# State-space layer: tokens reach rows (step, channel) and leave them through device memory in 256-byte runs; output products with the tables stationary

## The chip, the core and the metric

The kernel runs on one core of a Trainium2 chip. The time is that of one launch on the device, in microseconds (us). Before the change it is 2755.4 us, the median of three runs (2751.41, 2755.40 and 2757.46).

## What is computed

Two layers work on 1024 tokens of 1024 channels, in float32: RWKV-7 time mixing with its MLP, then an S5 state-space layer with its MLP. After each of the four parts the result is `layer_norm(sqrt(2) * h + f(h))`. The part around the change is the state-space layer: 64 groups of 16 channels, each of which drives 64 complex states by a diagonal recurrence.

```python
# s5_mix, cut: u is (token, group g, channel c), s a complex state per (group g, p)
s[t] = abar * s[t-1] + einsum('gc,gpc->gp', u[t], bbar)
y[t] = einsum('gp,gcp->gc', s_re[t], c_re) - einsum('gp,gcp->gc', s_im[t], c_im)
y = gelu(y + x * d_skip)
z = y @ w_glu
return z[..., :d] * sigmoid(z[..., d:])
```

## The kernel before

Activations lie channel-major: a tile holds 128 channels by 512 tokens, eight tiles `h[0..7]` make one half of the sequence, and the two halves are called A (H = 0) and B (H = 1). Each dense product is made of three float32r matmuls (`mm3`; all appear as L188 in the profile): a weight piece of 128 x 512 numbers is loaded into `wraw` (two buffers), copied by ScalarE into `whi`, and its remainder is made by VectorE in `wlo` (three buffers each; L148 and L149 are the helper lines of this split). One such piece is the stationary operand of four steps of the contraction, three matmuls each with `whi` or `wlo`.

The program is written as a sequence of Python calls with ranks; a planner orders each engine's instructions by rank and by a simulated time line. Every engine then takes its own queue strictly in that order. All DMAs are issued from the queue of SyncE (SP). Low ranks go first: layer norms have 99000, the state-space layer has 99300 (half A) and 99400 (half B), the building of its tables has 99500, and the dense MLPs have ranks from 200000 up. So the MLP of one half fills TensorE while the state-space layer of the other half goes through its chain:

1. `s5_tables` (L1010) makes three tables in device memory, interleaved with the first MLP: `tB` (input to state, per step), `tC` (state to output) and `tT` (input to output inside a block of eight steps). `tT` comes from `kpad`, a zero-padded tile of 16 taps, of which a window shifted by the step is stored.
2. `layer_norm(hA, 1, 0)` and then `s5(0, hA)`; the filler is `mlp(0, 1, hB)`, of which 12 of 16 steps stand ahead of `glu(0, hA)` in the program.
3. `layer_norm(hB, 1, 1)` and `s5(1, hB)`; the filler is `mlp(1, 0, hA)`, of which 13 steps stand ahead of `glu(1, hB)`.

Inside `s5` a half of 512 tokens is seen as 64 blocks of SL = 8 steps. The products want rows (step, channel): 8 steps x 16 channels of one group on 128 partitions, with the 64 blocks along the free axis. That form, `ug`, is reached by two rounds of transposes on TensorE. The first (`turn`, L154 for the upper and L156 for the lower half of the output) takes every eighth column of `h` and fills `u1` through `pu1` (copied at L1172). The second (L1179) turns each group of `u1` and is copied into `ug` at L1181. Then `pbu` (L1190) multiplies with `tB` into `hb`, and `advance` (L1200 to L1206, on VectorE and GpSimd) runs the recurrence over the blocks.

The output products have the tokens stationary: at L1234 `ug` (128 rows x 64 blocks) is the stationary operand and 128 columns of `tt` move, read with a step of four elements; at L1239 `hb` (64 rows x 64 blocks) is stationary and 128 columns of `tcm` move. The result has blocks on partitions, is copied to `y1` (L1241) and turned back to channels by a third round of transposes (`pyt`, L1247). VectorE adds `d * h` (L1249, in and out with a step of eight), ScalarE applies the gelu (L1251) and the tile is stored (L1252, `scr["y"]`). `glu` loads it again (L930) and splits it into operands for two dense products per output tile; L1000 and L1001 form the gated sum in `h`.

Elsewhere, `gate_c` in the first layer uses a constant tile `pick` (two 128 x 128 selectors; L355 to L360), and `h` comes from rings of eight buffers (`htile`).

In the profile one fp32 matmul appears as two records, each with its own weight load (PEld); a transpose made with `PE.transpose` appears as one.

Of the kernel before, what the change touches and what calls it, by code (L numbers as in the profile page):

```python
# [8 lines left out]
F32 = mybir.dt.float32  # L9
# [9 lines left out]
HT = 512  # L19
KT = 8  # L20
# [12 lines left out]
TB = 2  # L33
LN8R = 400000
# [36 lines left out]
def trunk(ctx, tc, A):  # L71
# [165 lines left out]
    pick = cp.tile([128, 2, 128], F32, name="pick")  # L237
    for j in range(2):
        V.tensor_copy(pick[:, j].rearrange("p (q n) -> p q n", q=4),
                      ident[:, 64 * j : 64 * j + 32].unsqueeze(1).broadcast_to([128, 4, 32]))  # L240

    def rwkv_proj(H):
# [9 lines left out]
        for k in range(KT):  # L252
            t = ap.tile([128, HT + 1], F32, tag="xs", name="xs", bufs=8)
# [95 lines left out]
        def gate_c():  # L349
# [3 lines left out]
            S.copy(e, p)  # L353
            p = psd()
# [472 lines left out]
    def htile(H):  # L827
        if H == 0:
            return ap.tile([128, HT + 1], F32, tag="xs", name="hA", bufs=8)[:, 0:HT]
        return sp.tile([128, HT], F32, tag="hB", name="hB", bufs=8)  # L830

    def layer_norm(h, gi, H, split_out=True):
# [41 lines left out]
        for k, t in enumerate(h):  # L874
            V.tensor_mul(t, t, pr)
            S.activation(t, t, AF.Identity, bias=vec(b, k), scale=vec(g, k))
            if split_out:
                ops.append(operand(t, H, G if k in LNG else V))
# [112 lines left out]
    def glu(H, h):  # L991
        ys = yload(H)
        for n in range(KT):
# [7 lines left out]
            V.scalar_tensor_tensor(h[n], h[n], ALPHA, s, op0=ALU.mult, op1=ALU.add)  # L1001
# [4 lines left out]
    tT = dr.tile([KT, 128, 2, 512], F32, name="tT")  # L1006
# [3 lines left out]
    def s5_tables():  # L1010
# [78 lines left out]
        kpad = pp.tile([128, 16, 16, 4], F32, name="kpad")  # L1089
        G.memset(kpad, 0.0)  # L1090
        for f in range(KT):
# [18 lines left out]
            def expand(out, src, npow, neg):  # L1110
# [15 lines left out]
            expand((ca[:, :, 0], ca[:, :, 1]), (bc[:, 1, 0], bc[:, 1, 1]), 9, True)  # L1126
            expand((bp[:, :, 0], bp[:, :, 1]), (bb[:, 0], bb[:, 1]), 8, False)
# [9 lines left out]
            for par in range(2):  # L1137
                ps_ = slice(64 * par, 64 * par + 16)
                S.copy(kpad[ps_, 8:].rearrange("p t c g -> p g (t c)"), p[ps_])
            tv = tT[f].rearrange("(s c) two n -> two c s n", c=16)  # L1140
            for par in range(2):
                src = kpad[64 * par : 64 * par + 16, 1:9].rearrange("p t c g -> p (t c g)")
                SP.dma_start(tv[par], bass.AP(src.tensor, src.offset, [src.ap[0], (64, SL), src.ap[1]]))
# [13 lines left out]
    def s5(H, h):  # L1157
# [6 lines left out]
        for f2 in range(4):  # L1164
            u1 = s5p.tile([128, 8, SL, 16], F32, tag="u1", name="u1", bufs=2)
# [214 lines left out]
```

## Time and profile before

| | |
|---|---|
| median of three runs | 2755.4 us |
| the profiled execution | 2756.91 us |
| its span, first to last instruction | 2755.1 us |
| mean granted TensorE clock | 0.958 |
| PE / PEld busy | 94% / 76% |
| DVE / ACT / POOL busy | 66% / 42% / 23% |
| PE's share of the chain that ended last | 63% |
| DMA: packets, volume | 215058, 345.90 MB |
| packets under 512 B | 21184 |

A group of instructions in the profile reads: line, engine, operation, output<-inputs, for a matmul rows*columns of the stationary operand, then out<-moving shape, xcount | busy time in us, mean ns of one | idle time of the engine just before them and what ended it. "SPq" is the queue that issues the DMAs. A matmul's record contains its latency, so records overlap; the busy time of a group is the union of its records.

### The profile page before, as it was taken

The numbers are of one execution on the slowest core, as the hardware profiler recorded it, in microseconds if no ns is written. First come the engines' busy times: TensorE is split into PE (matmuls) and PEld (weight loads), VectorE is DVE, ScalarE is ACT, GpSimd is POOL, SyncE is SP. The second block draws the span as 40 slices with busy tenths as digits, with TensorE's granted clock in tenths as the row PEclk, the third lists the DMA queues.
The fourth block names the chain that finished last, engine by engine and source line by source line (L and its number), as shares of the span: only waits on it lengthen the run. The fifth ranks groups of instructions, "written<-read, shape, count | busy, mean of one in ns | idle before, by whom it ended". The sixth has DMA issues, their size and how long they took to land.

```text
span 2755.1 us, 43773 instructions
## 1 busy us (share of the span) xinstructions
PE 2602.8 (94%) x16582; PEld 2099.3 (76%) x16582; DVE 1811.4 (66%) x3191; ACT 1156.3 (42%) x2038; POOL 628.2 (23%) x515
## 2 busy tenths in 40 slices
PE   7999879899899999889999999999999999999997
PEld 5778767678777877667877788778778887788886
DVE  7477676477788767997658554574765546855556
ACT  7455574554453333344432332344223324433333
POOL 3120642341334212332122000120220001210101
PEclk9989979899879999999999999999999999999999
DMA  4765455465222334564233533233343332333333
GB/s 146 234 206 164 153 180 153 148 192 170 87 79 83 99 94 145 138 157 140 89 123 118 185 96 98 83 89 106 113 164 112 98 96 85 115 96 97 97 94 103
DMA packets 215058, 345.90 MB, mean 126 GB/s; under 512 B 21184, under 2 KB 75584, under 8 KB 214848
## 3 DMA queue, kind: packets, MB, share of 16 engines
q1 hardware_dynamic: 214848, 343.10, 40.2%
q8 instruction: 131, 2.15, 0.3%
q14 instruction: 79, 0.65, 0.1%
HBM read 279.06 MB, written 63.96 MB: 125 GB/s over the span
## 4 chain that ended last, share of the span: by engine, by line
PE 63%; DVE 12%; DMA 5%; issue 4%; ACT 2%; POOL 1%; SPq 0%; ACTq 0%; DVEq 0%; POOLq 0%
PE d L188 53%; DVE wlo L149 2%; DMA wraw<-in_mw_dram 2%; PE py L1234 1%; PE pA L580 1%; PE py L1239 1%; DMA yl<-s_y 1%; DVE hA L975 1%; PE pbu L1190 1%; PE pu L154 1%; PE pR L687 1%; PE pX L692 0%; POOL rl L959 0%; ACT whi L148 0%; DVE t L1202 0%
## 5 line engine op out<-in xcount | busy, mean ns | idle before, releaser
L148 ACT CAST whi<-wraw 128x512 fp32r<-128x512 f32 x668 | 413.6, 620 | 932.0 <-PE d L188 625.0
L149 DVE TENSOR_TENSOR wlo<-wraw,whi 128x512 fp32r<-128x512 f32 x668 | 497.8, 746 | 432.6 <-ACT whi L148 412.7
L188 PE MATMUL d<-qbuf,whi 128*128 128x512 f32 (+1 forms) x2112 | 655.0, 393 | 20.5 <-DVE hA L975 7.7
L188 PEld LDWEIGHTS d<-qbuf,whi 128*128 128x128 f32 x2112 | 390.7, 190 | 115.2 <-DVE hA L975 14.6
L188 PE MATMUL d<-qbuf,wlo 128*128 128x512 f32 (+1 forms) x1056 | 409.5, 390 | 9.5 <-DVE wlo L149 9.3
L188 PE MATMUL d<-oAh,whi 128*128 128x512 f32 (+1 forms) x960 | 394.4, 414 | 21.0 <-ACT ev L417 8.4
L959 POOL TENSOR_TENSOR rl<-rl 128x512 f32<-128x512 f32 x128 | 155.7, 1216 | 1084.4 <-ACT rl L958 1080.4
L188 PE MATMUL d<-oAl,whi 128*128 128x512 f32 (+1 forms) x960 | 390.6, 408 | 5.6 <-DVE oAl L149 5.6
L188 PE MATMUL d<-oAh,wlo 128*128 128x512 f32 (+1 forms) x960 | 390.2, 407 | 5.8 <-DVE wlo L149 3.4
L188 PE MATMUL d<-oBh,whi 128*128 128x512 f32 x704 | 278.6, 396 | 0.0
L188 PE MATMUL d<-oBh,wlo 128*128 128x512 f32 x704 | 277.7, 395 | 0.0
L188 PE MATMUL d<-oBl,whi 128*128 128x512 f32 x704 | 276.4, 393 | 0.0
L188 PEld LDWEIGHTS d<-qbuf,wlo 128*128 128x128 f32 x1056 | 200.0, 190 | 55.1 <-DVE wlo L149 13.6
L188 PEld LDWEIGHTS d<-oAh,whi 128*128 128x128 f32 (+1 forms) x960 | 188.0, 196 | 66.5 <-ACT ev L417 10.2
L188 PEld LDWEIGHTS d<-oAh,wlo 128*128 128x128 f32 (+1 forms) x960 | 188.2, 196 | 49.9 <-DVE wlo L149 5.1
L188 PEld LDWEIGHTS d<-oAl,whi 128*128 128x128 f32 (+1 forms) x960 | 188.4, 196 | 46.9 <-DVE oAl L149 7.8
L975 DVE TENSOR_TENSOR hB<-hB,d 128x512 f32<-128x512 f32 (+1 forms) x256 | 165.2, 651 | 70.7 <-PE d L188 67.9
L975 DVE TENSOR_TENSOR hA<-hA,d 128x512 f32<-128x512 f32 x240 | 162.3, 683 | 47.1 <-PE d L188 44.2
L188 PEld LDWEIGHTS d<-oBh,wlo 128*128 128x128 f32 x704 | 132.5, 188 | 32.1 <-issue 2.0
L188 PEld LDWEIGHTS d<-oBl,whi 128*128 128x128 f32 x704 | 132.6, 188 | 29.9 <-issue 0.9
L188 PEld LDWEIGHTS d<-oBh,whi 128*128 128x128 f32 x704 | 132.8, 189 | 28.2 <-issue 0.7
L149 DVE TENSOR_TENSOR qbuf<-rl,qbuf 128x512 fp32r<-128x512 f32 x128 | 95.7, 748 | 73.0 <-ACT qbuf L148 72.6
(373 smaller groups left out, 3818.1 us busy)
## 6 DMA issues: line engine op xcount, KB each, us to landing
wraw<-in_mw_dram SPq DMA_DIRECT2D x520, 256.0 KB, 2.7
wraw<-in_glu_dram SPq DMA_DIRECT2D x64, 256.0 KB, 2.6
low<-wlo SPq DMA_DIRECT2D x52, 256.0 KB, 2.7
wlo<-low SPq DMA_DIRECT2D x52, 256.0 KB, 3.5
wraw<-in_wk_dram SPq DMA_DIRECT2D x32, 256.0 KB, 3.6
wraw<-in_wr_dram SPq DMA_DIRECT2D x32, 256.0 KB, 3.6
wraw<-in_wv_dram SPq DMA_DIRECT2D x32, 256.0 KB, 4.2
yl<-s_y SPq DMA_DIRECT2D x32, 256.0 KB, 3.1
```

What stands on the lines that cost most here:

```text
L148: S.copy(hi, src)
L149: (e or V).tensor_sub(lo, src, hi.bitcast(F32))
L154: PE.matmul(out, x, idt, start=True, stop=True)
L188: bulk.append((PE.matmul(p, w, x, **kw).ins, x.shape[-1]))
L580: PE.matmul(pp[h][:, cc, i], D.KB[j][hs, u].rearrange("p j l -> p (j l)"), D.AR[j][hs, u].rearrange("p j l -> p (j l)"), start=True, stop= ...
L687: hop.append(PE.matmul(pR[hs, i], at[:, h, c, i, 0], vsa[:, cl, h, i], start=True, stop=True))
L959: G.tensor_mul(r, r, r)
L975: V.tensor_add(z, z, p)
L1190: PE.matmul(p[qs, g2, ri], tb[:, g2, ri, qs], u[:, 2 * g2 + par], start=True, stop=True)
L1234: PE.matmul(p[64 * j : 64 * j + 64, g2], ug[f][:, 2 * g2 + par], tv[:, par, g2], start=g2 == 0, stop=False, skip_group_check=True)
L1239: PE.matmul(p[64 * j : 64 * j + 64, g2], hb[qs, 4 * f + g2, ri, 0:NSC], tcm[qs, g2, ri], start=False, stop=ri == 1, skip_group_check=True)
```

## The change

- **Into rows (step, channel).** The layer norm ahead of `s5` (new argument `steps`) writes each normalised tile to a new buffer with its columns in order (step, block) instead of (block, step), and stores it to `tH` in device memory, eight stores of 256 KB per half. `s5` loads `ug` from there: per tile of four `f`, eight DMAs (one per step), each of 16 partitions x 32 runs of 64 numbers, which is 256 bytes. The transposes of L154, L156 and L1179 and the copies of L1172 and L1181 are gone.
- **Output products.** The tables are stationary: `tt` with 128 x 128, `tcm` with 64 x 128 for each parity; 64 columns of `ug` or `hb` move. The parities go to two PSUM banks.
- **Out of the rows.** Two copies per `f2` put the result into `y` (16 x 64 per partition), and eight DMAs store it to `tY`, each of 16 partitions x 16 runs of 256 bytes. The transposes of L1247 are gone; `d * h` and the gelu move into `glu`, on tiles in order (step, block). `glu` ends with one strided instruction per tile, into a new buffer, that restores the order of tokens.
- **Tables.** `tT` is laid out by partition, written from a larger `kpad` (four `f` together) by 16 DMAs for every four `f` (32 in all, 16 before) in runs of 512 bytes; the powers used for `tB` are taken in reversed order from `pwr`, eight small copies on ScalarE.
- **Buffers.** The rings of `h` have nine buffers; `pick` is no constant but is made in `gate_c`, each time, in a `wraw` buffer.

```diff
-    pick = cp.tile([128, 2, 128], F32, name="pick")
...
-            t = ap.tile([128, HT + 1], F32, tag="xs", name="xs", bufs=8)
+            t = ap.tile([128, HT + 1], F32, tag="xs", name="xs", bufs=9)
...
+            pick = wp.tile([128, 2, 128], F32, tag="wraw", name="pick", bufs=2)
+            for j in range(2):
+                V.tensor_copy(pick[:, j].rearrange("p (q n) -> p q n", q=4),
+                              ident[:, 64 * j : 64 * j + 32].unsqueeze(1).broadcast_to([128, 4, 32]))
...
+            if steps:
+                h[k] = htile(H)
+                S.activation(h[k].rearrange("p (s c) -> p s c", s=SL), t.rearrange("p (c s) -> p s c", s=SL),
+                             AF.Identity, bias=vec(b, k), scale=vec(g, k))
+                SP.dma_start(tH[H, k], h[k])
+                continue
...
     def glu(H, h):
-        ys = yload(H)
+        ys = []
+        for k in range(KT):
+            y = tp.tile([128, HT], F32, tag="m", name="yl")
+            SP.dma_start(y, tY[H, k])
+            V.scalar_tensor_tensor(y, h[k], vec("d", k), y, op0=ALU.mult, op1=ALU.add)
+            S.activation(y, y, AF.Gelu_apprx_tanh)
+            ys.append(operand(y, H))
...
-            V.scalar_tensor_tensor(h[n], h[n], ALPHA, s, op0=ALU.mult, op1=ALU.add)
+            z = htile(H)
+            V.scalar_tensor_tensor(z.rearrange("p (c s) -> p s c", s=SL), h[n].rearrange("p (s c) -> p s c", s=SL), ALPHA,
+                                   s.rearrange("p (s c) -> p s c", s=SL), op0=ALU.mult, op1=ALU.add)
+            h[n] = z
...
+        pwr = pp.tile([128, 8, 2, 32], F32, name="pwr")
+        for j in range(8):
+            S.copy(pwr[:, j], pw[:, 7 - j])
+        kpad = pp.tile([128, TBF, 4, 16, 16], F32, name="kpad")
...
+            if f % TBF == TBF - 1:
+                for par in range(2):
+                    for s in range(SL):
+                        SP.dma_start(
+                            tT[16 * s : 16 * s + 16, par, f - TBF + 1 : f + 1].rearrange("c f g n -> c (f g) n"),
+                            kpad[64 * par : 64 * par + 16, :, :, 8 - s : 16 - s].rearrange("c f g t e -> c (f g) (t e)"))
...
+        for f in range(KT):
+            if f % UF == 0:
+                u = s5p.tile([128, 8 * UF, NSC], F32, tag="ug", name="ug", bufs=KT // UF)
+                for s in range(SL):
+                    SP.dma_start(u[16 * s : 16 * s + 16],
+                                 tH[H, f : f + UF, :, NSC * s : NSC * s + NSC].rearrange("f (g c) n -> c (f g) n", g=8))
+            ug.append(u[:, 8 * (f % UF) : 8 * (f % UF) + 8])
...
-                        PE.matmul(p[64 * j : 64 * j + 64, g2], ug[f][:, 2 * g2 + par], tv[:, par, g2],
+                        PE.matmul(pp[par][:, j, g2], tt[:, par, g2], ug[f][:, 2 * g2 + par],
...
-                            PE.matmul(p[64 * j : 64 * j + 64, g2], hb[qs, 4 * f + g2, ri, 0:NSC], tcm[qs, g2, ri],
+                            PE.matmul(pp[par][:, j, g2], tcm[qs, g2, ri], hb[qs, 4 * f + g2, ri, 0:NSC],
...
+            y = s5p.tile([128, 16, NSC], F32, tag="u1", name="yg", bufs=2)
+            for par in range(2):
+                S.copy(y.rearrange("p (f g r) n -> p r f g n", f=2, r=2)[:, par], pp[par])
+            for s in range(SL):
+                SP.dma_start(tY[H, 2 * f2 : 2 * f2 + 2, :, NSC * s : NSC * s + NSC].rearrange("f (g c) n -> c (f g) n", g=8),
+                             y[16 * s : 16 * s + 16])
```

In the new loop of the output products the parity is the innermost index of both product loops, and the loop over the two `f` of a pair is the outermost.

102 lines of the change are left out of this document (34 added, 68 removed).

## The prediction, on record before the result

> **What bounds the kernel now.** I read the page first: the busy shares, then the chain that ended last.
>
> ```profile
> PE 2602.8 (94%) x16582; PEld 2099.3 (76%) x16582; DVE 1811.4 (66%) x3191; ACT 1156.3 (42%) x2038; POOL 628.2 (23%) x515
> ...
> PE 63%; DVE 12%; DMA 5%; issue 4%; ACT 2%; POOL 1%; SPq 0%; ACTq 0%; DVEq 0%; POOLq 0%
> ```
>
> TensorE is the bound on average, but an average says nothing of the state-space stages. So next the busy time by windows, cut where the state-space layer of half A starts (1340), where its scan starts and ends (1420, 1495), where its last tile leaves (1556), and for half B its scan (1950 to 2023).
>
> ```profile
> core 0: us, PE busy (x) PEld busy (x) DVE busy (x) ACT busy (x) POOL busy (x), PEclk, DMA share, GB/s
> 1340.00:1420.00 80.00, 80.00 (x646) 64.85 (x646) 36.69 (x56) 34.55 (x59) 7.83 (x7) 1.00 0.36 115
> 1420.00:1495.00 75.00, 67.55 (x302) 51.34 (x302) 67.05 (x114) 19.45 (x33) 23.46 (x12) 0.98 0.28 86
> 1495.00:1556.00 61.00, 60.93 (x522) 46.27 (x519) 29.25 (x39) 21.78 (x37) 7.64 (x5) 1.00 0.65 228
> 1556.00:1655.00 99.00, 99.00 (x435) 81.30 (x434) 52.87 (x81) 33.76 (x58) 9.70 (x10) 1.00 0.34 102
> 1950.00:2023.00 73.00, 65.72 (x284) 50.18 (x284) 65.44 (x111) 19.47 (x33) 21.17 (x12) 0.98 0.29 87
> ```
>
> The reader is to see two kinds of stage. Ahead of the scan, and after it, PE never rests (80.00 of 80, 60.93 of 61, 99.00 of 99): a microsecond of TensorE work taken out there is a microsecond of the end. Only in the scan is PE short of work, by 7.5 and 7.3 us, with VectorE at 67.05 of 75 and 65.44 of 73; the change does not touch the scan.
>
> Then: is the chain of the state-space layer itself late for anyone? On the time line the last `y` of half A is stored here, and the first gated weights are issued here:
>
> ```profile
> 1554.59 0.33 SPq L1252 DMA_DIRECT2D s_y<-yg  x1
> ```
>
> ```profile
> 1654.91 5.99 SPq L169 DMA_DIRECT2D wraw<-in_glu_dram  x3
> ```
>
> There are 100 us between the two, filled with MLP products. So latency added to the chain is free up to that, and what counts is TensorE work, and whatever makes TensorE wait at the head of its queue.
>
> **TensorE's part of the change.** The groups of PE by line, from 1340 to 2090, which holds both halves:
>
> ```profile
> L1234 PE MATMUL py<-tt,ug 128*64 128x128 f32 x256 | 40.4, 408 | 0.1
> L1239 PE MATMUL py<-tcm,hb 64*64 64x128 f32 x512 | 31.9, 273 | 0.0
> L1190 PE MATMUL pbu<-ug,tb 128*64 128x64 f32 x512 | 16.7, 224 | 0.0
> L154 PE MATMUL pu<-ident,hB 128*64 128x128 f32 x64 | 9.6, 295 | 0.0
> L154 PE MATMUL pu<-ident,hA 128*64 128x128 f32 x64 | 9.6, 295 | 0.0
> L1247 PE MATMUL pyt<-ident,y 64*128 64x64 f32 x128 | 8.1, 229 | 0.0
> L1179 PE MATMUL pu<-ident,u 64*128 64x64 f32 x128 | 8.1, 229 | 0.0
> L156 PE MATMUL pu<-ident,hB 128*64 128x128 f32 x32 | 4.6, 272 | 0.0
> L156 PE MATMUL pu<-ident,hA 128*64 128x128 f32 x32 | 4.6, 272 | 0.0
> ```
>
> *Transposes.* All of L154, L156, L1179 and L1247 go: 9.6 + 9.6 + 4.6 + 4.6 + 8.1 + 8.1 = 44.6 us. Busy time includes the tail of each burst's last record, which lies beside the next burst; for some sixteen bursts at 0.16 us (a record below lasts 0.39 and the next starts 0.23 later) that is 2.6 us. I take **-42**.
>
> *What limits the new products.* Their moving side shrinks from 128 to 64 columns, their stationary side grows to 128 columns, so the weight load has to be priced. The closest shape is L580 of the first layer: 64 rows x 128 columns stationary, 128 columns moving. Two stretches of the time line, the first with the dense products just ahead, and one of L520:
>
> ```profile
> 926.34 0.39 PE L188 MATMUL d<-oAh,whi 128*128 128x512 f32 x1
> 926.34 0.19 PEld L188 LDWEIGHTS d<-oAl,whi 128*128 128x128 f32 x1
> ...
> 926.57 0.39 PE L188 MATMUL d<-oAl,whi 128*128 128x512 f32 x1
> ...
> 926.88 0.98 PEld L580 LDWEIGHTS pA<-AR,KB 64*128 64x128 f32 x16 [0.35 <-issue]
> ```
>
> ```profile
> 557.94 0.96 PEld L580 LDWEIGHTS pA<-AR,KB 64*128 64x128 f32 x8
> ```
>
> ```profile
> 85.66 1.08 PEld L520 LDWEIGHTS pss<-hsel,sq 128*128 128x128 f32 x8
> ```
>
> One load lasts 0.19. Eight in 0.96 are (0.96 - 0.19) / 7 = 0.110 us apart; sixteen in 0.98 are 0.053 apart. I read the second as two row halves loading and running side by side, since the loop alternates them, and the first as one half alone. L520 moves only 2 columns, so nothing but loading can hold it, and its loads come (1.08 - 0.19) / 7 = 0.127 apart, start of the burst included: a full 128 x 128 load takes about 0.11 whatever moves.
>
> *L1234* becomes 256 loads of 128 x 128 with no second half to pair: 256 x 0.110 = 28.2, with burst starts 29, against 40.4: **-11**. Bounds: 256 x 0.127 = 32.5 (-8), and 256 x 0.053 = 13.6 (-27) if loading did not limit. I take the value of the full load, because L520's row is that load.
>
> *L1239* becomes 512 records of 64 x 128 whose row halves alternate by parity, innermost: 512 x 0.053 = 27 at best (-5), 512 x 0.110 = 56.3 if one half at a time (+24). With burst starts, as now, I take 31: **-1**. L1190 does not change.
>
> The Trainium skill, page "TensorE: Matmul & The Clock Gate", Part 3, says that weight loads overlap running matmuls only where the row group differs; by it each full load of L1234 would add to its own moving time. The trace disagrees for the dense products: the load of the next one starts with the running one (both 926.34) and the next matmul follows 0.23 later, on the same rows. I keep it as a rival with a small chance.
>
> Sum for TensorE: -42 - 11 - 1 = **-54**.
>
> **The other engines.** From the groups of VectorE and ScalarE in the same window:
>
> ```profile
> L1249 DVE SCALAR_TENSOR_TENSOR yg<-hA,pv,pyt 128x512 f32<-128x512 f32 x8 | 9.6, 1195 | 7.1 <-DMA s_y<-yg 3.6 <-PE pyt L1247 3.5
> ...
> L1001 DVE SCALAR_TENSOR_TENSOR hA<-hA,sgl 128x512 f32<-128x512 f32 x8 | 5.5, 684 | 0.0
> ```
>
> ```profile
> L1172 ACT COPY u<-pu 128x512 f32<-128x512 f32 x16 | 9.3, 582 | 21.2 <-PE pu L154 21.2
> L1241 ACT COPY y<-py 128x512 f32<-128x512 f32 x16 | 9.2, 588 | 34.6 <-PE py L1239 23.9 <-POOL t L1204 10.7
> L1181 ACT COPY ug<-pu 128x512 f32<-128x512 f32 x16 | 8.6, 590 | 10.1 <-PE pu L1179 10.1
> ```
>
> VectorE swaps strides: the sum with `d` becomes contiguous (1195 to about 684 ns) and the last step of `glu` becomes strided (684 to about 1195), sixteen times each: 0. ScalarE loses L1172 and L1181, 18 us; L1241 remains as two copies per pair; the gelus only move. Neither engine was the bound around these stages, so I count nothing; if VectorE's cover went, the strided sums would cost at most 16 x 0.51 = 8 us.
>
> **Queues and waits that it adds.** Every DMA is issued by SP, and weights queue behind. Who holds SP now:
>
> ```profile
> SPq L169 <- DVE wlo L149: 1258.8, 518, 7.9
> ...
> SPq L930 <- DMA s_y<-yg: 30.4, 15, 4.2
> ```
>
> ```profile
> L764 SPq DMA_DIRECT2D s_y<-gt x16: 360/377/425, 307.9 to 1066.5; - x16
> ...
> DMA to landing us min/median/max: 2.3/2.6/4.1
> ```
>
> SP mostly waits for a free weight buffer: loads are issued as early as buffers allow. The change adds, per half, 8 stores of `tH`, 16 loads of `ug` and 32 - 8 stores of `tY`: 48; with 16 more for `tT`, 112 issues. L764 (512 runs of 512 bytes) has 0.377 for an issue and 2.6 us to landing. One weight piece feeds 4 x 3 products, 12 x 0.23 = 2.8 us of PE; two raw and three split buffers hold more than 5 us of work, so a burst of eight issues, 3.0 us, is covered.
>
> Three things may show. The products of L1190 now stand behind a store, eight issues and a load (2.6 + 3.0 + 2.6 = 8.2 us) for each of four `ug` tiles, at high rank: where the planner's idea of that is short, PE waits, with the MLP's products queued behind; bounds 0 and 8.2, I take 1 each, as the nearest wait on a landing, L930's, is 2.0 us (30.4 / 15) against the plan: **+4**. `pick` takes a weight buffer twice, until its copies and matmuls are through; no row shows that hold, and I bound it by 0 and twice L930's wait, 4 each, and take **+2** in all, since the weights stand two pieces ahead. The tables get eight small copies, each under 0.59 us (L1241), and 16 issues at 0.377, beside the first MLP: 0 to 10, I take **+2**. That makes +8.
>
> **The rivals.**
>
> *One half at a time.* If the planner or the array does not pair the row halves, L1239 costs 56.3 instead of 31: 25 more, 2736. For it: the stretch at 557.94. Against: the parity is innermost and both halves of `hb` are ready together.
>
> *Loading does not limit.* L1234 at 13.6 and L1239 at 27: 20 less, about 2691. Against it: L520.
>
> *No overlap on the same rows*, the page's rule as a mechanism of this kernel: L1234 at 256 x (0.110 + 0.053) = 41.7, 13 more, 2724.
>
> *PE waits for `ug`.* All of 8.2 us, four times, and not 4 us: 29 more, 2740.
>
> *SP starves the weights: slower.* The place is SP's queue in the state-space stages. Per half, two `ug` tiles hold it for 2.6 + 3.0, eight waits for `tH` or `tY` to land for 2.0 each, and four bursts of `tY` for 3.0: 39; the two bursts of `tT` 6.0 each: 90 us in all. It turns slower than before once more than 54 of these 90 (less the other +8, 46) reach PE; with three quarters exposed it is 2757 - 54 + 8 + 68 = 2779. Against it: a single hold is under 6 us and the buffers cover about that.
>
> The Trainium skill, page "DMA: Bandwidth & Descriptors", Specifications, says that transfers under 512 bytes are done as read-modify-write; by it the stores of `tY` would take longer to land than L764's 2.6 us, and the waits ahead of `glu` would grow. No row here shows a store in runs that short. It speaks against the change and for this rival; the 100 us of slack stand between.
>
> **How the numbers follow.** The profiled execution took 2756.9 us (span 2755.1), 1.5 above the median of the runs shown. 2756.9 - 54 + 8 = 2710.9; less one for the median, I say 2710. Chances: forecast 0.58, one half at a time 0.13, loading does not limit 0.08, no overlap 0.04, PE waits for `ug` 0.07, SP starves 0.10. The range 2688 to 2745 takes in all but the last. A measurement of this kernel can tell 0.2%, 5.5 us, from no change. Only the last rival lies above; a mild form of it, or two others together, could end within 0.2%: faster 0.86, same 0.04, slower 0.10.
>
> **What would show it.** Right: no PE group under the three transposes; the table products at about 29 us for 256 records and the state products at about 31 for 512; PE still full ahead of and after the scan; `glu` of half A starting some 27 us earlier against the end of its layer norm. Wrong: state products near 56; PE idle ahead of L1190 with a DMA of `ug` as releaser; SP held by landings of `tH` or `tY` while ScalarE waits for `wraw`; a total above 2745 with the PE groups as said.

## The result: 2845.5 us, slower by 3.5%

The kernel after took 2845.5 us (median of 4 runs, 2842.4 to 2849.8) against 2753.4 us of the kernel before beside it (4 runs, 2739.8 to 2757.5): ratio 1.0348, 95% interval 1.0326 to 1.0369 (the two medians alone give 1.033). The forecast was 2710 us. In lines of the kernel after, L188 is now L190, L148/L149 are L150/L151, L169 is L171, L1190 is L1204, L1234 is L1247 and L1239 is L1254.

The page after, busy shares and chain:

```profile
span 2840.7 us, 43002 instructions
...
PE 2609.8 (92%) x16134; PEld 2093.4 (74%) x16134; DVE 1831.8 (64%) x3193; ACT 1140.3 (40%) x2014; POOL 630.8 (22%) x515
...
PE 42%; DVE 5%; DMA 3%; SPq 2%; ACT 1%; issue 1%; POOL 0%; ACTq 0%; DVEq 0%; POOLq 0%
```

TensorE has 448 records fewer, exactly those of the transposes (128 + 64 + 128 + 128), and yet is busy 7 us longer. The span grew by 85.6 us, so the other 78.6 are time in which TensorE stands idle. SP's queue (SPq), 0% of the chain before, now has 2%. The output and input products from 1340 to 2110:

```profile
L1254 PE MATMUL py<-hb,tcm 64*128 64x64 f32 x512 | 43.1, 346 | 0.0
L1247 PE MATMUL py<-ug,tt 128*128 128x64 f32 x256 | 41.2, 331 | 20.0 <-DMA tt<-tT 20.0
L1204 PE MATMUL pbu<-ug,tb 128*64 128x64 f32 x512 | 21.1, 253 | 16.2 <-DMA ug<-tH 8.1 <-DMA wraw<-in_mw_dram 8.1
```

The transposes are gone, as forecast. But the two product groups that were to take 29 and 31 us take 41.2 and 43.1, and 36 us of waits stand ahead of L1247 and L1204, where there were 0.1 before. Three separate causes come out of the traces.

**1. Dense products that the change does not touch are slower, from the start of the kernel.** Windows of 50 us in the last MLP, TensorE fully busy with L188 (L190) alone; the columns are start and end, length, TensorE's busy time and number of records, granted clock, DMA share, GB/s. Before:

```profile
2600.00:2650.00 50.00, 50.00 (x221) 1.00 0.32 97
```

After:

```profile
2600.00:2650.00 50.00, 50.00 (x216) 1.00 0.33 95
```

216 products in the time of 221 at the same full clock: 231.5 ns from start to start instead of 226.2. Over the kernel, taking the records of 512 columns whose next record starts 200 to 260 ns later (some 7600 in each kernel), they came 228.5 ns apart before and 233.2 after.

**2. SP's queue is held.** Time line of SP after, two stretches (start, duration):

```profile
1263.32 0.34 SPq L171 DMA_DIRECT2D wraw<-in_mw_dram  x1
1263.74 21.00 SPq L1167 DMA_DIRECT2D tT<-kpad  x16
1284.84 2.79 SPq L171 DMA_DIRECT2D wraw<-in_mw_dram  x2
...
1371.45 4.26 SPq L1194 DMA_DIRECT2D ug<-tH  x6
1377.17 11.62 SPq L1194 DMA_DIRECT2D ug<-tH  x8
```

The sixteen stores of the tables hold the queue for 21.0 us, 1.31 each; eight loads of `ug` hold it for 11.62, 1.45 each. No weight is issued meanwhile. ScalarE, which splits the weights, shows it behind the first of the two: it stood idle for 16.92 us until a weight landed.

```profile
1289.62 0.62 ACT L150 CAST whi<-wraw 128x512 fp32r<-128x512 f32 x1 [16.92 <-DMA wraw<-in_mw_dram]
```

**3. The output products run at half clock.** Time line of PE after, in half A (the brackets give the idle time ahead):

```profile
1485.01 7.36 PE L1254 MATMUL py<-hb,tcm 64*128 64x64 f32 x128
1492.30 2.00 PE L1247 MATMUL py<-ug,tt 128*128 128x64 f32 x16
1503.01 3.68 PE L1247 MATMUL py<-ug,tt 128*128 128x64 f32 x16 [8.71 <-DMA tt<-tT]
...
1522.17 7.09 PE L1254 MATMUL py<-hb,tcm 64*128 64x64 f32 x64
1529.20 0.79 PE L190 MATMUL d<-oBh,wlo 128*128 128x512 f32 x1
```

The granted clock ahead of the wait and behind it (after the length: PE, PEld, DVE, ACT and POOL with their records, then the clock):

```profile
1485.00:1494.30 9.30, 9.30 (x145) 9.08 (x144) 0.07 (x1) 2.36 (x3) 4.67 (x2) 1.00 0.73 198
1503.00:1529.30 26.30, 25.04 (x177) 24.38 (x177) 4.31 (x7) 4.35 (x9) 0.00 (x0) 0.50 0.77 214
```

128 records in 7.36 us and 16 in 2.00 are the forecast pace, at a granted clock of 1.00. After the 8.71 us wait 16 take 3.68, and 64 take 7.09: nearly twice as long per record, at a granted clock of 0.50. This lasts until dense products follow at 1529, although TensorE is busy for 25.04 of the 26.30 us.

### The profile page after: what moved, and what is told of

Same layout as the page of the kernel before. It is cut to its first block, busy times and chain, and to the rows that moved or that the text cites. A ratio compares the mean times of both kernels' runs of the same rounds, so it can differ in the third digit from the quotient of the medians.

```text
span 2840.7 us, 43002 instructions
## 1 busy us (share of the span) xinstructions
PE 2609.8 (92%) x16134; PEld 2093.4 (74%) x16134; DVE 1831.8 (64%) x3193; ACT 1140.3 (40%) x2014; POOL 630.8 (22%) x515
## 4 chain that ended last, share of the span: by engine, by line
PE 42%; DVE 5%; DMA 3%; SPq 2%; ACT 1%; issue 1%; POOL 0%; ACTq 0%; DVEq 0%; POOLq 0%
PE d L190 40%; DMA wraw<-in_mw_dram 1%; DVE wlo L151 1%; SPq L1194 1%; SPq L1167 1%; DMA tY<-yg 1%; SPq L1260 1%; PE py L1247 1%; DVE t L1216 1%; PE py L1254 1%; DMA yl<-tY 1%; DVE hB L984 0%; DMA tt<-tT 0%; DVE hA L984 0%; ACT hB L881 0%
## 5 line engine op out<-in xcount | busy, mean ns | idle before, releaser
L150 ACT CAST whi<-wraw 128x512 fp32r<-128x512 f32 x668 | 413.8, 620 | 1046.4 <-PE d L190 758.9
L151 DVE TENSOR_TENSOR wlo<-wraw,whi 128x512 fp32r<-128x512 f32 x668 | 506.3, 759 | 455.6 <-ACT whi L150 444.5
L190 PE MATMUL d<-qbuf,whi 128*128 128x512 f32 (+1 forms) x2112 | 667.9, 399 | 42.7 <-DVE hA L984 18.2
L190 PEld LDWEIGHTS d<-qbuf,whi 128*128 128x128 f32 x2112 | 396.2, 192 | 146.8 <-DVE hA L984 23.3
L190 PE MATMUL d<-oAh,whi 128*128 128x512 f32 (+1 forms) x960 | 394.3, 415 | 38.5 <-ACT whi L150 20.2
L190 PE MATMUL d<-qbuf,wlo 128*128 128x512 f32 (+1 forms) x1056 | 418.1, 398 | 7.2 <-DVE wlo L151 7.0
L968 POOL TENSOR_TENSOR rl<-rl 128x512 f32<-128x512 f32 x128 | 149.6, 1169 | 1173.7 <-ACT rl L967 1111.5
L190 PE MATMUL d<-oAl,whi 128*128 128x512 f32 (+1 forms) x960 | 393.8, 412 | 3.1 <-DVE oAl L151 3.1
L190 PE MATMUL d<-oAh,wlo 128*128 128x512 f32 (+1 forms) x960 | 392.1, 410 | 4.6 <-DVE wlo L151 4.3
L190 PE MATMUL d<-oBh,whi 128*128 128x512 f32 x704 | 283.1, 402 | 0.0
L190 PE MATMUL d<-oBl,whi 128*128 128x512 f32 x704 | 281.2, 399 | 0.0
L190 PE MATMUL d<-oBh,wlo 128*128 128x512 f32 x704 | 279.8, 398 | 0.0
L190 PEld LDWEIGHTS d<-oAh,whi 128*128 128x128 f32 (+1 forms) x960 | 186.5, 196 | 88.7 <-ACT whi L150 21.4
L190 PEld LDWEIGHTS d<-qbuf,wlo 128*128 128x128 f32 x1056 | 202.5, 192 | 58.2 <-DVE wlo L151 11.3
L190 PEld LDWEIGHTS d<-oAh,wlo 128*128 128x128 f32 (+1 forms) x960 | 186.7, 195 | 52.0 <-DVE wlo L151 6.6
L190 PEld LDWEIGHTS d<-oAl,whi 128*128 128x128 f32 (+1 forms) x960 | 186.4, 195 | 48.0 <-DVE oAl L151 5.4
L190 PEld LDWEIGHTS d<-oBh,wlo 128*128 128x128 f32 x704 | 133.4, 190 | 34.4 <-issue 1.2
L190 PEld LDWEIGHTS d<-oBh,whi 128*128 128x128 f32 x704 | 133.7, 190 | 32.6 <-issue 0.9
L190 PEld LDWEIGHTS d<-oBl,whi 128*128 128x128 f32 x704 | 133.6, 190 | 32.5 <-issue 1.4
L151 DVE TENSOR_TENSOR qbuf<-rl,qbuf 128x512 fp32r<-128x512 f32 x128 | 95.1, 743 | 69.2 <-ACT qbuf L150 68.7
```

Source lines behind the costliest of these rows:

```text
L150: S.copy(hi, src)
L151: (e or V).tensor_sub(lo, src, hi.bitcast(F32))
L190: bulk.append((PE.matmul(p, w, x, **kw).ins, x.shape[-1]))
L968: G.tensor_mul(r, r, r)
```

## The experiments

Times are medians; beside each group of runs the kernel before took 2745.4 to 2749.1 us. Of e3, e12 and e17 there is one execution each, and only its trace is used. "Distance" below is the address of the moving operands `oAh`, `oAl` and `qbuf` less that of the weight buffers, in the compiled program; `oBh`, `oBl` lie 64 bytes further. The traces do not hold addresses, but the distances follow from the sizes: a ninth buffer of 2080 = 8 x 256 + 32 bytes adds 32 modulo 256, and each added tile its own size.

**Addresses.** A ring of nine instead of eight `xs` tiles of 2052 bytes (2080 with padding) puts everything behind it in another place. Four kernels move only that:

```diff
 e1: before, e2: after
-    ap = ctx.enter_context(tc.tile_pool(name="ap", bufs=1))
+    ap = ctx.enter_context(tc.tile_pool(name="ap", bufs=1)); V.memset(ap.tile([128, 8], F32, name="shim"), 0.0)
 e5: after, with [128, 24]; e10: after, with [128, 56] and mhalf [128, 16] for [128, 64]
```

> The kernel before with one added tile of 32 bytes at the head of the pool that holds the matmuls' moving operands; all of them then start at 32 modulo 64 bytes, as they do after the change, where a ring of nine buffers of 2080 bytes stands ahead of them. Nothing else changes. Theory (address): the median spacing of two dense matmuls goes from 227 to 234 ns, and with some 8,000 of them the time rises by 40 to 60 us, to about 2800. Rival (traffic or clock): the slower dense matmuls come from the added transfers or from the throttle, so this kernel stays at 227 ns and 2755 us.

> The changed kernel with the same added tile of 32 bytes, which brings the moving operands back to multiples of 64 bytes. Theory (address): dense spacing 227 ns, and 35 to 60 us less than the changed kernel, so about 2795, still slower than before by some 40, which is the part of SP's queue. Rival (traffic or clock): no change, 2845 and 234 ns.

> The kernel after, with a tile of 96 bytes ahead of the moving operands instead of 32, so that they start where they started in the kernel before: at a multiple of 128 bytes. Address theory: the start-to-start time of the 128x512 products was 227 ns in the kernel before (0 modulo 128), 234 in the kernel after (32 modulo 64), 231 with the 32-byte tile (64 modulo 128); it comes back to 227, and with 8100 of them the time is 20 to 30 us under the 2818 of the aligned kernel, about 2795. Rival: the remainder by 64 is all that counts and the 231 come from the denser DMA traffic; then it stays at 231 and 2818.

> The kernel after with a tile of 224 bytes ahead of the moving operands (and 192 bytes taken from a constant that is not used in full, to make room), so that the distance from the weight buffers to the moving operands is a multiple of 256 bytes, as in the kernel before. Distance theory, from the records matched to their addresses: the start-to-start time of the 128x512 products goes with the distance modulo 256 (mean ns of the records under 260): 0: 226.9; 32: 232; 64: 228 to 229; 96: 233; 128: 231 to 232; 192: 233; the start address itself does not count (a shift of weights and operands together by 64 changed nothing). Then the mean comes back from 232.3 in the kernel after to 227.6, and 7640 such records are 36 us: 2845 to about 2809. Rival: it goes with something else that moved with the buffers, such as the start address modulo 128 of the operands; then it is 229.4 as with the 32-byte tile, 2818.

| kernel | distance modulo 256 | mean ns, oA and qbuf / oB | time, us |
|---|---|---|---|
| before | 0 | 228.0 / 229.3 | 2747 |
| e1, before + 32 bytes | 32 | 233.2 / 233.3 | 2774.8 |
| after | 32 | 233.2 / 233.3 | 2845.5 |
| e2, after + 32 bytes | 64 | 229.4 / 232.4 | 2818.4 |
| e5, after + 96 bytes | 128 | 232.4 / 233.4 | 2836.2 |
| e10, after + 224 bytes | 0 | 228.0 / 229.5 | 2813.5 |

The same window of e1, and then of e10:

```profile
2600.00:2650.00 50.00, 50.00 (x216) 1.00 0.32 95
```

```profile
2600.00:2650.00 50.00, 50.00 (x221) 1.00 0.33 99
```

A tile of 32 bytes that nothing reads makes the kernel before 28 us slower (1.0100, 1.0074 to 1.0125), with the 216 records of the kernel after. 40 to 60 had been expected, and 4.7 ns on some 7600 records would be 36, so part of it presumably falls where the dense products do not set the time. The first idea, that the operands' start modulo 64 or 128 counts, fell with e5: a multiple of 128 as before, and yet 18 us slower than e2. Sorting the records by address gave the distance: 64 costs 229.3 to 229.5 on average wherever it occurs (e2's oA, oB of before and e10), 128 costs 232.4 twice (e2's oB, e5's oA). At 64 this is a mean of unlike products: in the kernel before, the products of `oBh` with `whi`, of `oBl` with `whi` and of `oBh` with `wlo` took 231.3, 227.0 and 229.4 ns to the start of the next, in e2 those of oA 229.0, 228.9 and 230.0. So the distance goes with the mean, and what sets the single products apart is open. e10, run as a test of that, came back to 221 records and to 2813.5 us, near the 2809 expected. (The expectations count some records in that follow closer than 200 ns, so their means are about 1 ns lower.) A shift of weights and operands together by 64 bytes (in e3 below) left 228.1 and 229.2. So the address costs the change some 32 us between the medians of after and e10, and 28 in e1. Why the distance matters was not shown.

**What a DMA costs the queue.** e3 puts blocks of eight DMAs by themselves ahead of the kernel before (extra work, not part of what is computed):

> The kernel before with DMAs added ahead of all its work, on an idle core, each kind eight in a row: loads of 128 KB as 16 partitions of 256-byte runs (the new loads), 16 partitions of 4096-byte runs, 128 partitions of 256-byte runs, one load of 1 MB as 128 partitions of 256-byte runs; stores of 64 KB from 16 partitions in 256-byte runs (the new token stores) and of 128 KB in 512-byte runs, from the same 16 partitions each time (the new table stores) and from other 16 partitions each time. The time of the whole says nothing. Theory (partitions): a transfer that touches 16 partitions is slow whatever its runs: 1.2 us and more apart for both 16-partition loads, at most 0.7 for the 128-partition load. Rival (runs): both 256-byte loads are equally slow, and the 4096-byte load is fast (0.4). For the stores the first theory says that the two of 512 bytes differ, the second that they are equal.

```profile
0.78 5.78 SPq L108 DMA_DIRECT2D l16x<-in_xT_dram  x8
15.68 3.58 SPq L113 DMA_DIRECT2D l16x<-in_xT_dram  x8
25.57 4.25 SPq L118 DMA_DIRECT2D l128x<-in_xT_dram  x8
32.65 0.85 SPq L122 DMA_DIRECT2D l128x32x<-in_xT_dram  x1
44.28 3.82 SPq L128 DMA_DIRECT2D sH<-s16x  x8
54.33 8.77 SPq L134 DMA_DIRECT2D sT<-s16x  x8
71.28 5.38 SPq L140 DMA_DIRECT2D sT<-s16y  x8
```

L134 is the tables' store (16 rows, 16 runs of 512 bytes each), all eight out of the same 16 partitions: 1.10 us each even alone. Out of eight different blocks of 16 partitions (L140) it is 0.67, in runs of 256 bytes (L128) 0.48. One DMA over 128 partitions and 32 runs of 256 bytes (L122), as much as eight pieces of 16 partitions, holds the queue for 0.85. The first block, the shape of `ug` (L108), contains the start of the kernel, so its 0.72 us each is an upper bound.

For the loads neither expectation held as a whole. Sixteen partitions in runs of 4096 bytes (L113) took 0.45 us each, near the rival's 0.4, where the theory had 1.2 and more; 128 partitions in runs of 256 bytes (L118) took 0.53, so short runs alone are not slow either. For the stores the theory's sign came out: two shapes that differ only in the partitions they read differ by 0.43 us. The shape of `ug` by itself held the queue for no more than 0.72 us; why it is 1.45 in the kernel, where other transfers run beside it, stays open.

**The holds.** e4 (32-byte tile) orders the rows (channel, step), so that a load of `ug` covers 128 partitions; e6 (32-byte tile) stores the tables for each `f`.

```diff
 e4
-                for s in range(SL):
-                    SP.dma_start(u[16 * s : 16 * s + 16], ...)
+                for i in range(UF):
+                    SP.dma_start(u[:, 8 * i : 8 * i + 8], tH[H, f + i].rearrange("(g c) (s n) -> (c s) g n", g=8, s=SL))
 e6
-            if f % TBF == TBF - 1:
-                ... tT[16 * s : 16 * s + 16, par, f - TBF + 1 : f + 1]
+            ... tT[16 * s : 16 * s + 16, par, f]
 e7, e8, e9: S.dma_start for the stores of tT and tY (e11: of tY); e9, e11: G.dma_start(y, tY[H, k])
```

> The changed kernel, aligned as in the run before it, with rows in order (channel, step): the loads of tokens then are eight per half, each over all 128 partitions, in the same 256-byte runs, and not sixteen over 16 partitions each. Tables are permuted to match. Theory (SP's queue is held by 16-partition transfers): the hold ahead of the state products (16 us per half) shrinks to some 4, and the time falls by 10 to 30 us against the aligned one. Rival (the run length holds the queue): no change, within 5 us.

> The kernel after with the 32-byte tile, and the tables' row layout stored in 16 small stores for each f (4 runs of 512 bytes a row) instead of two bursts of 16 for four f at a time. Queue theory: the two bursts held SP for 19.7 us each and left TensorE without weights; now no single hold exceeds 8 us, and the time falls by 10 to 25 us from 2818, to about 2800. Rival: what counts is the number of issues, 128 instead of 32; then SP is held for some 40 us in all instead of 39 and the time stays at 2818 or rises to 2830.

e4 took 2797.1 (21 less than e2, the intervals 1.0151 to 1.0218 and 1.0228 to 1.0292 apart), e6 2802.9 (15 less). In e6 a burst of 16 stores now holds the queue for 7.4 to 8.9 us. The hold of `ug` is shown as a cost. For the tables e6 alone would not do, as its interval (1.0174 to 1.0271) overlaps e2's; but TensorE's waits for `whi` fall from 33.7 to 20.7 us, and e16 below has a larger step.

> The kernel after with the 32-byte tile, and the stores of the tables and of y issued by ScalarE, which makes the data, instead of by SyncE: the same transfers, on another queue. Queue theory: weights are no longer behind them, the waits of ScalarE for a raw weight buffer in the two bursts go, and the time falls by 25 to 40 us from 2818, to about 2785. Rival 1: the transfers themselves are the load (DMA engines), then no change, 2818. Rival 2: ScalarE is held instead for the 20 us of a burst, and with it the weight split that it does; then it is as slow as before or slower, 2818 to 2840.

> The kernel before this one (the 32-byte tile, stores of the tables and of y on ScalarE) with one more edit: the loads of y ahead of glu are issued by GpSimd instead of SyncE. Head-of-line theory: on SyncE each pair of these loads waits for its stores to land, and the table load of the next products stands behind it; TensorE then waits 8.5 us, its clock falls to 0.5, and the table products, which are bound by their weight loads, do not bring it back, so that they run at half rate until dense products follow. With the loads elsewhere the wait of L1247 on tt falls from 20 to under 5 us, 256 records at 112 ns come back to 30 us and 512 at 56 ns to 31 us, and the time falls by 25 to 45 us from 2816, to about 2780. Rival: the clock falls because the product block itself is too thin, whatever precedes it; then the wait goes but the block stays at half rate, and only about 15 us are won, 2800.

e7 took 2815.8, no gain over e2: ScalarE is held instead (TensorE's two longest waits for it are 12.8 and 11.9 us), and on SP the loads of `y`, waiting for their stores, stand ahead of a table load:

```profile
1471.39 0.53 SPq L1237 DMA_DIRECT2D tt<-tT  x1
1472.87 0.34 SPq L1239 DMA_DIRECT2D tcm<-tC  x1
1480.73 0.80 SPq L1004 DMA_DIRECT2D yl<-tY  x2
1481.58 0.53 SPq L1237 DMA_DIRECT2D tt<-tT  x1
```

e9 moves those loads to GpSimd. The wait of L1247 for `tt` falls from 17.7 to 10.4 us in sum, the longest from 8.5 to 4.2, and yet the time is 2828.4, 13 more. PE in e9, then SP:

```profile
1469.24 7.36 PE L1254 MATMUL py<-hb,tcm 64*128 64x64 f32 x128
1477.74 3.64 PE L1247 MATMUL py<-ug,tt 128*128 128x64 f32 x16 [1.15 <-DMA tt<-tT]
1483.28 3.67 PE L1247 MATMUL py<-ug,tt 128*128 128x64 f32 x16 [1.89 <-DMA tt<-tT]
1486.88 7.09 PE L1254 MATMUL py<-hb,tcm 64*128 64x64 f32 x64
```

```profile
1499.74 12.91 SPq L1198 DMA_DIRECT2D tb<-tB  x4
```

Here a wait of 1.15 us was enough for half pace (3.64 us for 16), and it stays. And a new hold has taken the place of the old: four loads for the next half, waiting for table buffers, stand 12.91 us ahead of the weights, and TensorE's waits for `whi` grow from e7's 28.6 us to 44.5. So the theory of e7 and e9 fell. e9's rival was right that the block stays at half pace, but not on its 15 us; since the waits shrank and did not go, e9 cannot say whether the block would slow down without any, and e12 below answers that.

> All of it together: operands at a multiple of 128 bytes, rows (channel, step) so that the loads of ug cover 128 partitions, and the stores issued by ScalarE. If the three causes add: 2797 less 25 for the address, less 30 for the queue, about 2745, a little under the kernel before. If the lasting cost is elsewhere (TensorE's clock after its idle stretches, or the strided step of the layer norm), about 2770 to 2780.

> All together: distance 0 modulo 256, rows (channel, step), tables stored for each f by SyncE, y stored by ScalarE and loaded by GpSimd. If the causes add: 2818 less 14 for the distance, 21 for the rows, 15 for the tables, 30 for the table loads: 2738, under the kernel before's 2747. If the product block stays at half rate: 2755.

Both combinations missed their sums: e8 2813.9 (its 96 bytes make the distance 128, at 232.4 ns), e11 2805.8 where 2738 or 2755 had been expected. With the output side as changed, no median went below 2797.

**Which forms keep the clock.** e12 and e17 put blocks of products ahead of the kernel before (extra work), behind rests of some 18 us (the expectations say 14) or behind 64 dense products.

> The kernel before with a block of work ahead of it: after rests of some 14 us, 64 dense products, then 192 products of the form of L1247 (128x128 stationary, 64 columns moving), 192 of the form of the kernel before's L1234 (128x64 stationary, 128 columns moving), 384 of L1254's form and 384 of L1239's form; then the same four again, each right behind 64 dense products. All of it is extra and is not part of what is computed; the total says nothing. Theory, from the traces: the clock stays at 0.5 through a block of the new forms however long, as it did for six full windows of 3.4 us in the kernel after, and falls or holds behind dense products only through waits; the forms of the kernel before, with twice the moving columns, bring it to 1.0 within some 7 us. So L1247's form at 213 ns throughout from cold, L1234's form faster after the first windows. Rival: every form that keeps TensorE busy brings the clock back within two windows, and what held it down in the kernel after were the short waits for tt; then L1247's form goes from 213 to 112 ns after some 7 us.

> The kernel before with three blocks ahead of it, each after a rest of some 14 us and so from a half clock: 192 products of L1247's form; eight times 16 of L1247's and 32 of L1254's form, as the output products of the kernel after run; eight times 16 of L1234's and 32 of L1239's form, as in the kernel before. Extra work, not part of what is computed. From the blocks before: L1254's and L1239's forms (64 rows) stayed at half rate for 82 us from a half clock and at full rate for 43 us behind dense products, while L1234's form came to full rate within a few us. Theory: L1247's form stays cold or the mixture with L1254 does, for the whole block (some 8 times 5.2 us), and the old mixture comes to full rate at its first run of L1234. Rival: L1247's form too brings the clock back by itself within 7 us and the new mixture runs warm; then only the waits kept it down in the kernel after.

Windows of e12 (busy and number for PE, PEld, DVE, ACT, POOL; then the granted clock): L1234's form from rest, L1254's from rest, L1239's from rest, and behind dense products L1247's and L1254's:

```profile
98.00:121.00 23.00, 22.20 (x380) 22.20 (x382) 1.24 (x2) 0.00 (x0) 0.00 (x0) 0.92 0.01 2
139.00:221.00 82.00, 81.87 (x768) 81.90 (x768) 0.49 (x1) 0.00 (x0) 0.00 (x0) 0.50 0.00 1
239.00:320.00 81.00, 80.97 (x766) 81.00 (x768) 0.41 (x1) 0.00 (x0) 0.00 (x0) 0.50 0.01 1
359.00:400.00 41.00, 41.00 (x367) 40.92 (x365) 0.00 (x0) 0.00 (x0) 0.00 (x0) 1.00 0.00 1
...
496.00:539.00 43.00, 42.81 (x748) 42.67 (x747) 0.00 (x0) 0.00 (x0) 0.00 (x0) 1.00 0.01 2
```

Time line of PE in e17: 384 records of L1247's form from rest; the last run of the new mixture (L114 is L1247's form, L127 L1254's), 105 us into it; then the old mixture (L120 is L1234's form, L135 L1239's):

```profile
19.99 82.18 PE L114 MATMUL b<-bt 128*128 128x64 f32 x384 [19.99 <-DVE bt L102]
...
225.10 7.09 PE L127 MATMUL b<-bt 64*128 64x64 f32 x64
249.94 3.68 PE L120 MATMUL b<-bt 128*64 128x128 f32 x32 [17.75 <-DVE bt L102]
253.56 3.67 PE L135 MATMUL b<-bt 64*64 64x128 f32 x64
257.15 1.97 PE L120 MATMUL b<-bt 128*64 128x128 f32 x32
259.05 3.34 PE L135 MATMUL b<-bt 64*64 64x128 f32 x64
```

Both new forms hold a full clock behind dense products (367 records in 41 us, 112 ns each, at 359), so the block is not too thin by itself. But from rest they did not win it back: 82 us of L1247's form at 214 ns a record, 112 us of the mixture, without one wait. In e17 this is read from the pace, which is that of the kernel after at a granted 0.50 (16 in 3.68 us, 64 in 7.09): the trace of e17 has no clock record before 254.3 us, so its windows show 1.00 there. The old mixture is at full pace after two runs; L1234's form alone, from rest, had a mean of 0.92 over its window in e12, L1239's alone 0.50. One difference remains: these blocks read their moving operand without a step, L1234 in the kernel before with a step of four. The Trainium skill, page "TensorE: Matmul & The Clock Gate", Part 1, says that some 3.4 us of sustained matmuls release the clock, whatever they are; the runs here disagree for these forms (a granted 0.50 for 82 and 81 us in e12).

**One side at a time**, all at distance 0 (against e10):

```diff
 e13: e10 with the output loop and yload of the kernel before; e14: e10 with its transposes into ug
 e15: e13, rows (channel, step), tables stored for each f
 e16: e13, tables as before; u[16 * (SL - 1 - s) : 16 * (SL - s)] for u[16 * s : 16 * s + 16]
 e18: e16, rows (channel, step from the last); tH stored in reversed blocks, ug loaded over 128 partitions
```

> The kernel with the distance 0 modulo 256 (2813), with the output side of the kernel before: table products with the tables moving, transposes of y, y stored and loaded as there. Only the tokens' way into the rows goes through memory. If the output side is what costs (product block at half clock, 9 us waits for tt, stores of tY): 50 to 60 us less, about 2757, with only the stores of the tables and the loads of ug left. If the input side costs (table stores of 20 us, ug loads): about 2800.

> The kernel with the distance 0 modulo 256 (2813), with the input side of the kernel before: transposes of the tokens into rows, no tH, no loads of ug in pieces. The row layout of the tables (two bursts of 16 stores) stays. If the output side costs as the clock theory has it: about 2790 to 2810, since only the ug wait (8 us a half) goes and 27 us of transposes come back. If the input side is what costs: about 2770.

> The input side alone through memory (the output side by transposes as in the kernel before, with the last step of glu reading its gated products in the right order), distance 0 modulo 256, rows (channel, step) so that the loads of ug cover 128 partitions, tables stored for each f. If the gains of e4 (21) and e6 (15) add to the 2775 of the input side alone: about 2740, against 2749 of the kernel before. If they overlap, since both are the weights behind SyncE's queue: about 2760.

> The input side alone, distance 0 modulo 256, with the tables laid out and stored as in the kernel before (two stores for each f, no bursts of 16): the steps stand in reversed blocks in the rows, which the loads of ug place. Queue theory: the two bursts of 20 us cost some 15 to 30 us, so from 2775 to about 2750; the 8 us waits for ug, twice, remain. If the bursts cost nothing on this side: 2775.

> The input side alone with the tables stored as in the kernel before (2745, level with the kernel before), and the rows in the order (channel, step from the last), so that the loads of ug cover 128 partitions; for that the stores of tH place their eight blocks in reversed order. In the kernel before it TensorE waited 10.4 and 5.7 us ahead of L1193's products, and its clock was halved for some 20 us after the first; with the wide loads these waits were 3.1 us. If they are what eats the 27 us of transposes saved: 10 to 20 us less, about 2730, faster than the kernel before by some 0.6%. If the planner gives it back elsewhere: 2745.

In e13 the last step of `glu` takes its gated products in the wrong order of columns, so it does not compute the layer; e15, e16 and e18 have that right, and the step costs about the same (eight in 9.2 us in e13, 9.5 in e16). Times: e13 2775.4 (38 less than e10), e14 2814.7 (1 more), e15 2746.7 (0.9997 of before, 0.9978 to 1.0017), e16 2744.7 (0.9993, 0.9982 to 1.0004), e18 2733.7 (0.9962, 0.9948 to 0.9976).

So the output side costs 38 us, with its transposes saved already counted. Going back to the table layout and stores of before (e13 to e16, which also drops the copies to `pwr`) is worth 31. As a test of the two together, e14, with the new output side and the new table stores but the old input side, lies 66 above the kernel before; 38 and 31 make 69. With both back (e16) the input side is level with the kernel before.

In e16 much of what the transposes save goes into a wait that e18 does not have (L1193 and L1194, first of e16 and then of e18, are the L1190 of before, which took 16.7 us without a wait):

```profile
L1193 PE MATMUL pbu<-ug,tb 128*64 128x64 f32 x512 | 21.3, 254 | 16.2 <-DMA wraw<-in_mw_dram 16.2
```

```profile
L1194 PE MATMUL pbu<-ug,tb 128*64 128x64 f32 x512 | 19.6, 236 | 0.0
```

The profile names a weight as the releaser of the 16.2 us, but the wait is gone in e18, where above all the loads of `ug` are wider, so it was most likely for `ug`. e18 is faster than both kernels: 0.9962, which is some 10 us against the kernel before. The differences of the medians from after to e10, e13 and e16 (32, 38 and 31) add up to the 101 between after and e16 because they are one chain; their sum proves nothing, and in another order each could have another size.

**What the step of four cost.** e13 and e15 keep the tables laid out by partition, so the old output products there move `tt` without a step. L1234's products in e13 (L1242) and in e16 (L1237, the old layout), then 28 of them in one piece in the kernel before and in e13, all 28 at a granted clock of 1.00:

```profile
L1242 PE MATMUL py<-tt,ug 128*64 128x128 f32 x256 | 26.5, 312 | 7.3 <-DMA tt<-tT 6.5 <-ACT y L1249 0.7
L1237 PE MATMUL py<-tt,ug 128*64 128x128 f32 x256 | 40.8, 408 | 2.0 <-ACT y L1244 1.2 <-DMA tt<-tT 0.9
```

```profile
1421.94 3.84 PE L1234 MATMUL py<-tt,ug 128*64 128x128 f32 x28
```

```profile
1403.51 1.96 PE L1242 MATMUL py<-tt,ug 128*64 128x128 f32 x28
```

28 records take 1.96 us instead of 3.84, and the group 26.5 instead of 40.4 (27.3 in e15). So about half of L1234's price was the step of the moving read. The layout alone, with the tables still moving, takes off 14 us, more than the 11 that turning the operands was to bring, and keeps a form that wins the clock back. It also shifts what the steps above mean: both groups of output products together took 72.3 us in the kernel before, 63.2 in e13 and 73.6 in e16, so the 38 us are measured against faster output products than those of before, and the 31 contain their loss. No run has the layout alone in the kernel before.

## Why the prediction was wrong, point by point

Three steps failed: the buffers, a term put at nothing (some 32 us); the price of a DMA on SP's queue, and with it the tables (some 31); and the full clock that was taken for granted for the new output products (with their waits for `tt`, some 38). Behind them, the input side gave back what it saved.

- *TensorE is the bound, a microsecond there is one of the end.* Right: each of the three causes is TensorE slower or idle.
- *Transposes, -42.* Right as a term: the records that are gone are these. On the input side, whose share before the tails is 36.5 (the 27 in e18's expectation is too little), it was eaten, by the waits for `ug` above all, until e18, which is the only version that kept a part (some 10 us).
- *Dense products.* The sum has no term for them. The step that failed is the pricing of the buffers, which looked at `pick` alone and put the ninth `xs` buffer at nothing without a reason: that buffer moved every operand behind it. Measured: 4.7 ns on each of some 7600 records, which is 36 us, of which 28 (e1) to 32 us (after to e10) reach the end.
- *L1234 at 29 and L1239 at 31, -12 together.* The pace was right (16 in 2.00 us, 128 in 7.36) and so was the pairing of the row halves, so those rivals are out. The term is 41.2 + 43.1 = 84.3 instead of 60, because every price was taken at the full clock of the quoted windows, and it was not asked whether the new forms win it back after a wait. The comparison with 40.4 missed that half of that price was the step of four.
- *PE waits for `ug`, +4.* Measured 16.2 us for L1204, and 20.0 for `tt` ahead of L1247, which no step priced: the table load stood behind stores and loads of `y`.
- *Tables, +2, bounds 0 to 10.* Far too small: 31 us from e13 to e16, although e16 also gives up the tables without a step.
- *Issues at 0.377 us, a single hold under 6 us.* This is the step that failed on SP's side: the holds were 21.0 and 11.62. Only `tY`, eight in 5.11, stayed under 6. L764, the row that the price was taken from, reads 128 partitions in runs of 512 bytes; the new loads touch 16 partitions in runs of 256, and the table stores read the same 16 again and again. In e3 the two shapes alone held it for up to 0.72 and for 1.10, so the shape is a part of it and the place in the kernel the rest.
- *SP starves the weights, chance 0.10.* This rival came true in kind: SP held, ScalarE waiting for `wraw`. The time is above its 2779 because two causes came on top that it does not contain, the distance and the clock; its own price of 68 us was not measured by itself.
- *The stores of `tY` landing later than L764's 2.6 us.* They landed after 2.4 us (median of 64). That was not a cause.

## What to carry to other kernels

Look first at a group that the change does not touch: if its pace per record has moved, the buffers have, and the distance between stationary and moving operands should be put back before anything else is judged. Price a DMA by what it holds the queue for in its own shape and in a burst as long as the real one; a row of another shape (0.377 us here) can be nearly four times too low. If a product moves its operand with a step, try it without one before turning the product around. Ask of a new form of product whether it can win back the clock after a wait, and if not, give it no waits or let dense products follow closely.

## What was not expected of the hardware

- Products with a stationary operand of 128x128 and 512 moving columns (float32r) came 228.0 ns apart on average at distance 0 modulo 256 bytes between weights and moving operand, 229.3 to 229.5 at 64, 232.4 at 128, and 233.2 to 233.4 at 32, 96 and 192.
- fp32 products of 128x128 stationary with 64 moving columns stayed at half pace for 82 us without a pause (e17), the two forms with 64 rows at a granted clock of 0.50 for 82 and 81 us (e12); with 128 rows, 64 stationary columns and 128 moving columns full pace came back within one or two runs (7.2 us in e17, where products of 64 rows stand between).
- The same store costs SP's queue 1.10 us when eight of them read the same 16 partitions and 0.67 when each reads its own (one execution, e3).
- fp32 products of 128 rows, 64 stationary and 128 moving columns: 28 records took 3.84 us when the moving operand was read with a step of four, and 1.96 without.
